# A FoX/RWKV-7 layer on one core: two products a slot later, one sum queued behind the solve, the last pair turned by VectorE

## The chip, the cores and the metric

The kernel runs on one core of one Trainium2 chip. The metric is the device time of one execution in microseconds (us), as the median of several runs. The core has five engines that work side by side, each through its own queue in order: TensorE (PE, with its weight loads shown as PEld), VectorE (DVE), ScalarE (ACT), GpSimd (POOL) and SyncE (SP). In this kernel SP issues almost all transfers (DMA) between the chip's memory and the core's on-chip memory.

## The reference

One layer for 256 frames of width 4096, all in float32:

```python
proj = x @ w_in                                # 256 x 4096 times 4096 x 14544
fox_out  = forgetting attention, 16 heads of 128, from q, k, v, f
r, kr, vr, wd, ad = token shift of the rwkv columns
decay = exp(-exp(-softplus(-(w0 + tanh(wd) @ w_up)) - 0.5))
a     = sigmoid(a0 + ad @ a_up)
y     = RWKV-7 scan, 32 heads of 64, in 4 chunks of 64 frames
h     = concat(fox_out, groupnorm(y) + bonus) * silu(z)
x     = layernorm(ALPHA * x + h @ w_out)
```

The two big products are the input projection and the output projection. Between them stand 16 attention heads and 32 small recurrent heads whose state goes from chunk to chunk.

## The kernel before

**Main work.** Every float32 operand is split into a high and a low part, and a product is three passes on TensorE: high times high, low times high, high times low (L147 to L149 for the input projection, L880 to L882 for the output). The input columns are taken in eight pairs of heads, n = 0 to 7, and four blocks of 512 columns, b = 0 to 3, for each pair: b = 0 holds r and k of the recurrent heads, b = 1 the values, b = 2 and b = 3 the q, k and gate columns of one attention head each. A weight tile holds two of the 32 row groups (512 KB). SP loads it (L218), ScalarE makes its high part (L141) and VectorE its low part (L142). Four raw tiles, four high parts and three low parts can be held at once.

**Side work and slots.** All the rest runs as Python generators that are advanced while the program is traced. `slot()` (L197) advances each generator by one `yield`, and the main loop calls it after every six wide matmuls, so a block of 512 columns has 32 slots and a pair 128. What a generator traces in a slot is queued on VectorE no earlier than the newest low part. `yield from wait(k)` lets k slots go by. The order on the engines is then fixed by a planner that goes by trace order and by when it reckons operands to be ready; the chip plays that order as it is. `keep_in_program_order(x)` pins x behind the instruction traced just before it on the same engine, whatever that is; `issue_after(y)` queues what is traced within behind y on y's engine.

**The generators.** `ahead` runs `prepare(i)` for the 16 column groups in turn; its first part, `front(i)` (L417), splits the up-projection weights (L420, L422), forms the LoRA product `lp` on TensorE (L428 to L430), and yields three times. `prepare(2n)` begins a slot after pair n-1 is done, and after `front` it waits until r and k of its group have come in (`rk`). `chain` runs `rwkv(n)` for the eight pairs: Gram products `gp` (L534), a triangular solve of 31 steps on VectorE (L601 and L604, one step in a slot), transfers of the solved blocks (`td` L611, `T` L613), the sum over values `vm` (L616), eight `SV` writes (L623), and then for the four chunks c: residual `rh` (L647), its copies `R` (L650, VectorE and ScalarE), `up` (L678), its copies `UV` (L681), and for c < 3 the state update `sp` (L687). The readout `yp` follows (L707, L709), then normalisation and gating into h.

**Turning blocks.** `unload(n, b)` (L796) brings a block from frames-by-columns to columns-by-frames. For all but two blocks VectorE transposes it in 32 x 32 pieces (L809), four transfers write it to memory (`turn`, L281) and, for an attention head, four bring it back as q, k and the two gates. For b = 2 and b = 3 of the last pair, TensorE transposes it instead (`tr`, L835) and ScalarE copies the result (L837). Then `fox(i)` runs the head: scores (L743, L744), softmax, transposed weights `pT` (L759), output (L764, L765).

**The output projection** begins while the last heads are still worked on. Fourteen weight tiles of output block 0 and fourteen of block 1 come first, with one slot for every six matmuls, 56 in all; then the last four row groups (28 to 31), which belong to the last pair. Row groups below 29 went to memory (`hd`) and come back (`h`, L855); 29 to 31 stay on the chip (`hl`, L382).

Of the kernel before, what the change touches and what calls it, by code (L numbers as in the profile page):

```python
# [14 lines left out]
ALU = mybir.AluOpType  # L15
AX = mybir.AxisListType

P = 128
S = 256
# [5 lines left out]
HD = 64  # L25
# [17 lines left out]
LAND = 3  # L43
# [41 lines left out]
def layer(ctx: ExitStack, tc: tile.TileContext, xt, xtok, w_main, w_lora, w_first, muv, w_o, up, par, mulora, fbias, lng, lnb, cst, out):  # L85
    nc = tc.nc
# [8 lines left out]
    def pst(name):  # L95
        return ps.tile([P, 512], F32, tag="ps", name=name)
# [34 lines left out]
    ident = cs[:, C_ID : C_ID + P]  # L131
# [26 lines left out]
    for n, (k0, k1) in enumerate(pieces):  # L158
        for k in range(k0, k1):
            t = xpool.tile([P, 2, S], F32R, tag=f"x{k}", name=f"x{k}")  # L160
# [29 lines left out]
    def wait(n):  # L190
        for _ in range(n):
            yield
# [87 lines left out]
    def issue(out, src):  # L280
        tc.keep_in_program_order(nc.sync.dma_start(out=out, in_=src))  # L281

    def turn(src, name, each=2):
        _, m, cols = src.shape
        d = dram.tile([cols // B, B, m, 4, B], F32, tag=f"dt{m}_{cols}", name=name, bufs=2)
        s = src.rearrange("p m (q t) -> p m q t", t=B)
        for a in range(4):
            issue(d[:, :, :, a, :].rearrange("q i m t -> i m q t"), s[B * a : B * (a + 1)])
            if a % each == each - 1:
                yield  # L290
        return d
# [109 lines left out]
    vs_ = {}  # L401
# [15 lines left out]
    def front(i):  # L417
        upt = ups[i]
        uph = rp.tile([LORA, 2, P], F32R, tag="uph", name=f"uph{i}")
        nc.scalar.copy(flat(uph), flat(upt))  # L420
        upl = rp.tile([LORA, 2, P], F32R, tag="upl", name=f"upl{i}")
        nc.vector.tensor_tensor(flat(upl), flat(upt), flat(uph).bitcast(F32), ALU.subtract)  # L422
        load_up(i + 1)
        yield
        lp = pst(f"lp{i}")
        for j in range(2):
            o = lp[:, j * S : (j + 1) * S]
            nc.tensor.matmul(o, uph[:, j, :], lr[:, j, 0, :], start=True, stop=False)  # L428
            nc.tensor.matmul(o, uph[:, j, :], lr[:, j, 1, :], start=False, stop=False)
            nc.tensor.matmul(o, upl[:, j, :], lr[:, j, 0, :], start=False, stop=True)  # L430
        tw = rt(f"tw{i}")
        nc.scalar.activation(tw, lp[:, :S], AF.Tanh, scale=0.5, bias=half[:, 0, i : i + 1])
        ta = rt(f"ta{i}")
        nc.scalar.activation(ta, lp[:, S:], AF.Tanh, scale=0.5, bias=half[:, 1, i : i + 1])
        yield
        nc.vector.tensor_scalar(tw, tw, -0.5 * DECAY, -0.5 * DECAY, ALU.mult, ALU.add)
        L = rt(f"L{i}")
        nc.vector.tensor_tensor_scan(L, cs[:, C_SCAN : C_SCAN + S], tw, 0.0, ALU.mult, ALU.add)
        eL = rp.tile([P, NCH, C + 1], F32, tag="eL", name=f"eL{i}")
        nc.gpsimd.memset(eL[:, :, 0:1], 1.0)  # L440
        nc.scalar.activation(eL[:, :, 1:], ch(L), AF.Exp)
        eI = t256("eI", f"eI{i}")
        nc.scalar.activation(eI, L, AF.Exp, scale=-1.0)
        yield
        am = t256("am", f"am{i}")
        nc.scalar.activation(am, ta, AF.Identity, scale=hka[:, 0, i : i + 1], bias=hka[:, 1, i : i + 1])
        ae = t256("ae", f"ae{i}")
        nc.vector.scalar_tensor_tensor(ae, ta, 1.0, eI, ALU.add, ALU.mult)
        return eL, eI, am, ae
# [70 lines left out]
    def rwkv(n):  # L520
# [8 lines left out]
        for u in range(2):  # L529
            for c in range(NCH):  # L530
                for j in range(2):
                    h = HALF[j]
# [4 lines left out]
        p, t = bks[n], vs_[n]  # L537
# [10 lines left out]
        for u in range(2):  # L548
            for j in range(2):
                h = HALF[j]  # L550
# [15 lines left out]
        for u in range(2):  # L566
            v = flat(BK[:, u, : NCH - 1, :])
# [25 lines left out]
        prod = rp.tile([P, 2, NJ, B], F32, tag="prod", name=f"prod{n}")  # L593
# [5 lines left out]
        for t, s in enumerate(range(B - 2, -1, -1)):  # L599
            w = B - 1 - s  # L600
            first = nc.vector.tensor_tensor(prod[:, :, :, s + 1 :], nb[:, :, s : s + 1, s + 1 :].to_broadcast([P, 2, NJ, w]), xc[:, :, :, s + 1 :], ALU.mult)  # L601
            if not t or not n:
                tc.keep_in_program_order(first)
            nc.vector.tensor_reduce(xc[:, :, :, s : s + 1], prod[:, :, :, s:], AX.X, ALU.add)  # L604
            next(other, None)
            if t % ROWS == ROWS - 1:
                yield
# [5 lines left out]
                nc.sync.dma_start(out=T[B * a : B * (a + 1), u], in_=td[u, a].rearrange("c r s -> r c s"))  # L613
        vm = rp.tile([P, 2, 2, 2], F32, tag="vm", name=f"vm{n}")
        vt = vs_[n].rearrange("p m (u j v) -> p m u j v", u=2, j=2)
        tc.keep_in_program_order(nc.vector.tensor_reduce(vm.rearrange("p m u j -> p (m u j)"), vs_[n].rearrange("p m (a v) -> p (m a) v", v=HD), AX.X, ALU.add))  # L616
        yield
        for j in range(2):
            o = HALF[1 - j]
# [51 lines left out]
        for c in range(NCH):  # L671
            if c:
                R = residual(c)
                yield
            yield
            upp = pst(f"up{n}_{c}")
            for u in range(2):
                nc.tensor.matmul(upp[:, u * C : (u + 1) * C], X[:, u, c, :], R[:, u, :], start=True, stop=True)  # L678
            uv = upp[:, : 2 * C].rearrange("p (u t) -> p u t", u=2)
            for j in range(2):  # L680
                (nc.vector.tensor_copy if j else nc.scalar.copy)(UV[j][HALF[j], :, c, :], uv[HALF[j]])  # L681
            yield
            if c == NCH - 1:
                break
            sp = pst(f"sp{n}_{c}")
            for u in range(2):
                nc.tensor.matmul(sp[:, u * P : (u + 1) * P], BKt[:, u, c, :], flat(UVt[:, u, c]), start=True, stop=True)  # L687
            for j in range(2):
                h = HALF[j]
                if c == 0:  # L690
                    nc.vector.tensor_copy(SV[j][h, :, 1, :], diagonal(sp, j))
                else:
                    nc.vector.tensor_tensor(SV[j][h, :, c + 1, :], diagonal(sp, j), sl[h], ALU.add)
            if c < NCH - 2:
                sl = rp.tile([P, 2, C], F32, tag="sl", name=f"sl{n}_{c}")
                for j in range(2):
                    for u in range(2):
                        nc.scalar.mul(sl[HALF[j], u], SV[j][HALF[j], u, c + 1, :], lc[HALF[j], u, c + 1 : c + 2])
            yield from wait(2)
# [96 lines left out]
    def unload(n, b, bk, vt):  # L796
        yield from wait(LAG)
        if b == 0:
            while n and 2 * n - 1 not in prepared:
                yield  # L800
        elif b == 2:
            while n and n - 1 not in done:
                yield
        last = n == G // 2 - 1 and b > 1
        if b == 3 and not last:
            yield from wait(BEHIND)
        if not last:
            for m in range(2):
                nc.vector.transpose(bk[:, m, :], bk[:, m, :])  # L809
            yield from wait(2)  # L810
            d = yield from turn(bk, f"bt{n}_{b}")
            unloading.clear()
            yield
        if b == 0:
            for u in range(2):
                i = 2 * n + u
                while n and n - 1 not in bonned:
                    yield
                raw = rp.tile([P, 2, S], F32, tag="s2", name=f"raw{i}")
                issue(raw, turned_back(d[8 * u : 8 * u + 8]))  # L820
                yield from wait(LAND)
                for j in range(2):
                    rk[i, j] = shifted(raw[:, j, :], j, i)
            return
        i = 2 * n + b - 2
        while i and i - 1 not in foxed:
            yield
        fq, fk = t256("fq", f"fq{i}"), t256("fk", f"fk{i}")
        zf, zr = t256("szf", f"zf{i}"), t256("szr", f"zr{i}", 2)
        if last:  # L830
            for h, pair in enumerate(((fq, fk), (zf, zr))):
                tr = pst(f"tr{h}")
                for t in range(2):
                    for m in range(2):
                        nc.tensor.transpose(tr[:, t * S + m * P : t * S + (m + 1) * P], bk[:, m, (2 * h + t) * P : (2 * h + t + 1) * P], ident)  # L835
                for t in range(2):
                    nc.scalar.copy(pair[t], tr[:, t * S : (t + 1) * S])  # L837
                yield
            unloading.clear()
        else:  # L840
            for j, t in enumerate((fq, fk, zf, zr)):
                issue(t, d[4 * j : 4 * j + 4].rearrange("b i m a t -> (b i) (m a t)"))
                if j % 2:
                    yield
            yield from wait(LAND - 1)
        nc.scalar.mul(fq, fq, FOX_SCALE)
        side(fox(i, fq, fk, vt))
        yield
        silu2(zf, f"f{i}")
        silu2(zr, f"r{i}")  # L850
# [267 lines left out]
```

## Time and profile before

| | |
|---|---|
| median of 3 runs | 1921.72 us (1921.52 to 1923.91) |
| profiled execution | 1921.7 us, of which the span from first to last instruction is 1919.5 us |
| TensorE clock granted | 0.998 of full speed |
| PE, DVE, ACT, POOL busy | 1906.1, 1375.6, 987.3, 259.1 us |
| moved by DMA | 420.04 MB, 219 GB/s on average |

How to read it: a row of the timeline has the start in us, the length, the engine, the source line, the operation, the tiles out<-in, the shape, and how many were merged; what stands in brackets at the end is the idle time before it and who ended it. Matmuls overlap: two neighbours that start 0.23 us apart are each shown as 0.39 us long, so a start-to-start distance, not a length, is what a matmul costs. A delay that is shorter than the overlap shows as no idle time.

### The profile page before, as it was taken

To read this page: it belongs to the slowest core of one execution; us is meant where nothing else is said; L and a number is where in the kernel's file an instruction comes from. 1 tells how busy PE (TensorE), PEld (TensorE's weight loads), DVE (VectorE), ACT (ScalarE), POOL (GpSimd) and SP (SyncE) were. 2 spreads that over 40 slices of the span, in tenths; PEclk is the share of its full clock that TensorE was granted. 3 is DMA by queue.
4 is the path that set the end of the run, shared out by engine and by line. 5 is a ranking of instruction groups with operands and counts; after the bars stand their busy time and mean duration, and the time that the engine had idled before them with its cause. 6 is when DMAs were issued, how large, how long until landed. Compare 5 with 4: busy or idle time off the path is not lost.

```text
span 1919.5 us, 27983 instructions
## 1 busy us (share of the span) xinstructions
PE 1906.1 (99%) x9785; PEld 1583.1 (82%) x9785; DVE 1375.6 (72%) x2355; ACT 987.3 (51%) x1543; POOL 259.1 (13%) x463
## 2 busy tenths in 40 slices
PE   9999999999999999999999999999999999999998
PEld 9878788888888888888888888888888878888886
DVE  7677768776876688677867786778677856755555
ACT  6554555456545644564456454645474554434333
POOL 0022012111310131013101300140013001000000
PEclk9999999999999999999999999999999999999999
DMA  9577667867686768677766776677667876766564
GB/s 344 154 232 230 193 188 229 242 202 208 209 249 194 225 204 244 195 217 217 237 199 213 223 232 203 212 225 223 206 211 221 276 257 231 253 200 202 186 203 165
DMA packets 269393, 420.04 MB, mean 219 GB/s; under 512 B 142338, under 2 KB 169364, under 8 KB 269252
## 3 DMA queue, kind: packets, MB, share of 16 engines
q1 hardware_dynamic: 268820, 417.58, 70.2%
q8 instruction: 76, 1.25, 0.3%
q10 hardware_dynamic: 432, 0.69, 0.1%
q14 instruction: 65, 0.53, 0.1%
HBM read 388.55 MB, written 29.64 MB: 218 GB/s over the span
## 4 chain that ended last, share of the span: by engine, by line
PE 96%; DVE 2%; DMA 1%; ACT 1%; issue 0%; SPq 0%; DVEq 0%; ACTq 0%
PE acc L147 24%; PE acc L149 23%; PE acc L148 23%; PE oacc L882 6%; PE oacc L880 6%; PE oacc L881 6%; PE gp L534 1%; PE rh L647 1%; PE up L678 1%; PE sp L687 1%; PE accl L149 1%; PE accl L147 1%; DMA w<-in_w_main_dram 1%; PE accl L148 0%; PE yp L709 0%
## 5 line engine op out<-in xcount | busy, mean ns | idle before, releaser
L759 POOL COPY pT<-lg 32x96 f32<-32x96 f32 x128 | 59.6, 466 | 406.7 <-DVE lg L755 402.0
L571 POOL COPY BKt<-BK 32x192 f32<-32x192 f32 x128 | 76.8, 600 | 55.2 <-DVE BK L568 50.2
L604 DVE TENSOR_REDUCE xc<-prod 128x8 f32<-128x16 f32 (+30 forms) x248 | 72.2, 291 | 5.5
L601 DVE TENSOR_TENSOR prod<-Nb,xc 128x8 f32<-128x8 f32 (+30 forms) x248 | 72.1, 291 | 3.6
L142 DVE TENSOR_TENSOR w_6l<-w,w_6h 128x1024 fp32r<-128x1024 f32 x31 | 39.8, 1283 | 40.6 <-ACT w_6h L141 23.4
L142 DVE TENSOR_TENSOR w_14l<-w,w_14h 128x1024 fp32r<-128x1024 f32 x31 | 38.0, 1225 | 39.4 <-ACT w_14h L141 33.3
L141 ACT CAST w_13h<-w 128x1024 fp32r<-128x1024 f32 x31 | 32.6, 1052 | 45.8 <-issue 12.3
L141 ACT CAST w_12h<-w 128x1024 fp32r<-128x1024 f32 x31 | 32.6, 1051 | 45.8 <-PE acc L148 26.5
L142 DVE TENSOR_TENSOR w_8l<-w,w_8h 128x1024 fp32r<-128x1024 f32 x31 | 37.8, 1220 | 25.4 <-ACT w_8h L141 17.2
L142 DVE TENSOR_TENSOR w_13l<-w,w_13h 128x1024 fp32r<-128x1024 f32 x31 | 38.3, 1234 | 23.6 <-ACT w_13h L141 12.1
L142 DVE TENSOR_TENSOR w_7l<-w,w_7h 128x1024 fp32r<-128x1024 f32 x31 | 37.9, 1222 | 20.5 <-ACT w_7h L141 8.0
L142 DVE TENSOR_TENSOR w_12l<-w,w_12h 128x1024 fp32r<-128x1024 f32 x31 | 38.9, 1256 | 18.8 <-ACT w_12h L141 10.3
L142 DVE TENSOR_TENSOR w_5l<-w,w_5h 128x1024 fp32r<-128x1024 f32 x31 | 39.7, 1282 | 16.8 <-PE acc L149 10.5
L142 DVE TENSOR_TENSOR w_11l<-w,w_11h 128x1024 fp32r<-128x1024 f32 x31 | 38.2, 1232 | 18.0 <-issue 12.4
L141 ACT CAST w_9h<-w 128x1024 fp32r<-128x1024 f32 x31 | 32.5, 1050 | 35.9 <-PE acc L148 25.5
L142 DVE TENSOR_TENSOR w_3l<-w,w_3h 128x1024 fp32r<-128x1024 f32 x31 | 37.9, 1222 | 18.0 <-ACT w_3h L141 10.2
L147 PE MATMUL acc<-w_5h,x 128*128 128x512 f32 x124 | 50.6, 408 | 0.0
L147 PE MATMUL acc<-w_8h,x 128*128 128x512 f32 x124 | 50.5, 408 | 0.0
L149 PE MATMUL acc<-w_2l,x 128*128 128x512 f32 x124 | 48.4, 391 | 1.4 <-DVE w_2l L142 1.4
L147 PE MATMUL acc<-w_15h,x 128*128 128x512 f32 x124 | 49.6, 400 | 0.0
L147 PE MATMUL acc<-w_11h,x 128*128 128x512 f32 x124 | 49.1, 396 | 0.4 <-ACT w_11h L141 0.4
L147 PE MATMUL acc<-w_9h,x 128*128 128x512 f32 x124 | 49.5, 399 | 0.0
(812 smaller groups left out, 6605.1 us busy)
## 6 DMA issues: line engine op xcount, KB each, us to landing
w<-in_w_main_dram SPq DMA_DIRECT2D x496, 512.0 KB
wo<-in_w_o_dram SPq DMA_DIRECT2D x128, 512.0 KB
bt<-bk SPq DMA_DIRECT2D x88, 128.0 KB
Nb<-nd SPq DMA_DIRECT2D x16, 512.0 KB
hd<-hl SPq DMA_DIRECT2D x29, 256.0 KB
h<-hd SPq DMA_DIRECT2D x29, 256.0 KB
wr<-in_w_first_dram SPq DMA_DIRECT2D x15, 384.0 KB
lr<-in_w_lora_dram SPq DMA_DIRECT2D x14, 336.0 KB
```

The lines of the kernel that those rows point to most:

```text
L141: nc.scalar.copy(hi[:, :n], src[:, :n])
L142: latest[0] = nc.vector.tensor_tensor(lo[:, :n], src[:, :n], hi[:, :n].bitcast(F32), ALU.subtract)
L147: nc.tensor.matmul(acc[:, :n], xs[k][:, 0, tt], hi[:, o : o + n], start=(k == 0), stop=False)
L148: nc.tensor.matmul(acc[:, :n], xs[k][:, 1, tt], hi[:, o : o + n], start=False, stop=False)
L149: nc.tensor.matmul(acc[:, :n], xs[k][:, 0, tt], lo[:, o : o + n], start=False, stop=(k == KT - 1))
L571: nc.gpsimd.tensor_copy(BKt[B * b : B * (b + 1), :, :, B * a : B * (a + 1)], BK[B * a : B * (a + 1), :, : NCH - 1, B * b : B * (b + 1)])
L601: first = nc.vector.tensor_tensor(prod[:, :, :, s + 1 :], nb[:, :, s : s + 1, s + 1 :].to_broadcast([P, 2, NJ, w]), xc[:, :, :, s + 1 :], ...
L604: nc.vector.tensor_reduce(xc[:, :, :, s : s + 1], prod[:, :, :, s:], AX.X, ALU.add)
L759: (nc.gpsimd.tensor_copy if b % 2 else nc.scalar.copy)(pT[B * b : B * (b + 1), :, B * a : B * (a + 1)], lg[B * a : B * (a + 1), :, B * b : ...
L880: nc.tensor.matmul(acc, ht[k][:, 0, tt], hi, start=(k == 0), stop=False)
L881: nc.tensor.matmul(acc, ht[k][:, 1, tt], hi, start=False, stop=False)
L882: nc.tensor.matmul(acc, ht[k][:, 0, tt], lo, start=False, stop=(k == KT - 1))
```

## The change

- `front(i)`: two slots instead of one go by before the LoRA product is traced.
- `rwkv(n)`: a further slot goes by before each state update `sp`, for chunks 0 to 2.
- `vm` is queued behind the last step of the solve on VectorE, not behind the instruction that happens to be traced before it.
- `unload(7, 2)` and `unload(7, 3)` take the way of the other blocks: VectorE transposes, four transfers out and four back. The TensorE transposes and ScalarE copies go. The wait of 13 slots that the other b = 3 blocks have is still left out for the last.

```diff
@@ front @@
         load_up(i + 1)
-        yield
+        yield from wait(2)
         lp = pst(f"lp{i}")
@@ rwkv @@
-            nc.vector.tensor_reduce(xc[:, :, :, s : s + 1], prod[:, :, :, s:], AX.X, ALU.add)
+            solved = nc.vector.tensor_reduce(xc[:, :, :, s : s + 1], prod[:, :, :, s:], AX.X, ALU.add)
...
-        tc.keep_in_program_order(nc.vector.tensor_reduce(vm.rearrange("p m u j -> p (m u j)"), vs_[n].rearrange("p m (a v) -> p (m a) v", v=HD), AX.X, ALU.add))
+        with tc.issue_after(solved.ins):
+            nc.vector.tensor_reduce(vm.rearrange("p m u j -> p (m u j)"), vs_[n].rearrange("p m (a v) -> p (m a) v", v=HD), AX.X, ALU.add)
...
             if c == NCH - 1:
                 break
+            yield
             sp = pst(f"sp{n}_{c}")
@@ unload @@
-        if not last:
-            for m in range(2):
-                nc.vector.transpose(bk[:, m, :], bk[:, m, :])
-            yield from wait(2)
-            d = yield from turn(bk, f"bt{n}_{b}")
-            unloading.clear()
-            yield
+        for m in range(2):
+            nc.vector.transpose(bk[:, m, :], bk[:, m, :])
+        yield from wait(2)
+        d = yield from turn(bk, f"bt{n}_{b}")
+        unloading.clear()
+        yield
...
-        if last:
-            for h, pair in enumerate(((fq, fk), (zf, zr))):
-                tr = pst(f"tr{h}")
-                for t in range(2):
-                    for m in range(2):
-                        nc.tensor.transpose(tr[:, t * S + m * P : t * S + (m + 1) * P], bk[:, m, (2 * h + t) * P : (2 * h + t + 1) * P], ident)
-                for t in range(2):
-                    nc.scalar.copy(pair[t], tr[:, t * S : (t + 1) * S])
-                yield
-            unloading.clear()
-        else:
-            for j, t in enumerate((fq, fk, zf, zr)):
-                issue(t, d[4 * j : 4 * j + 4].rearrange("b i m a t -> (b i) (m a t)"))
-                if j % 2:
-                    yield
-            yield from wait(LAND - 1)
+        for j, t in enumerate((fq, fk, zf, zr)):
+            issue(t, d[4 * j : 4 * j + 4].rearrange("b i m a t -> (b i) (m a t)"))
+            if j % 2:
+                yield
+        yield from wait(LAND - 1)
```

## The prediction

> **What bounds the kernel now.** I read the page's busy times first, then the chain that ended last, then TensorE's waits.
>
> ```profile
> PE 1906.1 (99%) x9785; PEld 1583.1 (82%) x9785; DVE 1375.6 (72%) x2355; ACT 987.3 (51%) x1543; POOL 259.1 (13%) x463
> PE 96%; DVE 2%; DMA 1%; ACT 1%; issue 0%; SPq 0%; DVEq 0%; ACTq 0%
> ```
>
> ```profile
> PE acc L149 <- DVE w_2l L142: 1.4, 1, 1.4
> ```
>
> TensorE is busy 99% and carries 96% of the chain. The time is its queue: the wide passes, the small products between them, and the few moments in which it stands still. So each edit is worth what it takes out of or adds to the start-to-start distances on TensorE; VectorE (72%), ScalarE (51%) and the transfers matter only where they come late for it. The longest listed wait on other work is this one of 1.4 us; but the list is not all, since a delay below 0.16 us (0.39 long, 0.23 apart) hides in the overlap.
>
> **A. The TensorE transposes of the last pair go.**
>
> ```profile
> 1501.09 0.39 PE L149 MATMUL acc<-w_1l,x 128*128 128x512 f32 x1
> 1501.32 0.60 PE L835 MATMUL tr<-cs,bk 128*128 128x128 f32 x4
> 1501.67 0.48 PE L147 MATMUL acc<-w_1h,x 128*128 128x512 f32 x1
> 1501.99 0.40 PE L148 MATMUL acc<-w_1h,x 128*128 128x512 f32 x1
> ```
>
> From 1501.09 to the second wide pass after the group is 0.90; two plain distances would be 2 x 0.227 = 0.45. So four transposes cost 0.45 us. Two blocks in two halves make four such groups: 4 x 0.45 = **1.8 us less**, on the bounding engine, without doubt. [...]
>
> **B. `sp` a slot later.** A group of four 128-column products costs 0.45 when it waits for nothing (A). For `sp`:
>
> ```profile
> 1366.73 0.40 PE L149 MATMUL acc<-w_4l,x 128*128 128x512 f32 x1
> ```
>
> ```profile
> 1367.72 0.39 PE L148 MATMUL acc<-w_4h,x 128*128 128x512 f32 x1
> ```
>
> ```profile
> 1383.25 0.40 PE L149 MATMUL acc<-w_9l,x 128*128 128x512 f32 x1
> ...
> 1384.29 0.39 PE L148 MATMUL acc<-w_9h,x 128*128 128x512 f32 x1
> ```
>
> ```profile
>   DVE UV L681: 3.5, 13
> ```
>
> These are the wide passes around a group, in two places. The distances are 0.99 and 1.04, so the groups cost 0.54 and 0.59: 0.09 and 0.14 more than 0.45. The last line, the idle time before `sp`, says that 13 of the 24 groups wait for the `UV` copy. A slot is 6 x 0.227 = 1.36 us, far more, so the wait ends: 13 x 0.11 = **1.4 us less** (0 if it moves to the next product, 1.8 at 0.14 each). With `sp` go its `SV` writes on VectorE and the scaled copies on ScalarE, no transfer; the steps behind keep their distances, and each pair's chain gets 3 slots longer.
>
> **C. `lp` a slot later.**
>
> ```profile
>   DVE upl L422: 1.3, 6
> ```
>
> Six products waited 1.3 us in all for VectorE's low part of the up-projection. In B the waits showed half in the distances (13 x 0.11 of 3.5), so I take **0.4 us less**, between 0 and 1.3.
>
> **D. `vm` behind the solve.** In pair 0 it now runs among the solve's steps, and its `SV` writes with it:
>
> ```profile
> 208.17 0.68 DVE L616 TENSOR_REDUCE vm<-vs 128x8 f32<-128x512 f32 x1
> ...
> 214.66 1.22 DVE L142 TENSOR_TENSOR w_2l<-w,w_2h 128x1024 fp32r<-128x1024 f32 x1
> ```
>
> ```profile
> 214.09 0.39 PE L148 MATMUL acc<-w_2h,x 128*128 128x512 f32 x1
> 215.93 0.50 PE L149 MATMUL acc<-w_2l,x 128*128 128x512 f32 x1 [1.45 <-DVE w_2l L142]
> ```
>
> TensorE stood 1.84 - 0.23 = 1.6 us for a low part queued behind `vm` (0.68) and the eight `SV`. With these behind the solve the low part can come sooner; or the planner puts as much other work ahead of it. Between 0 and 1.6 I take **0.8 less**. ScalarE's copies of `SV` follow the same way, and no transfer does; in pair 7 `vm` already comes after the solve.
>
> **E. The stall of pair 7.**
>
> ```profile
> 1574.02 0.39 PE L880 MATMUL oacc<-wo_8h,h 128*128 128x512 f32 x1
> 1575.31 0.66 PE L678 MATMUL up<-R,X 128*128 128x64 f32 x4 [0.90 <-ACT R L650]
> ```
>
> ```profile
> 1575.00 0.26 ACT L650 COPY R<-rh 64x128 f32<-64x128 f32 x1
> ```
>
> Here `R` comes at 1575.00 on ScalarE, which the last attention head's copies and a cast have held before; 1.29 - 0.23 = 1.1 us. That head comes 7 slots later by the new transfers, the recurrent chain 9 to 12, so this meeting dissolves or another takes its place: 0 to 1.1, I take **0.6 less**.
>
> **F. What the change adds.**
>
> ```profile
> L809 DVE STREAM_TRANSPOSE bk<-bk x44: 660/694/714, 73.9 to 1412.8; 128x512 f32<-128x512 f32 x44
> ```
>
> VectorE gets four of these transposes (median 694 ns), ScalarE loses eight copies; neither is near its limit. SP gets eight writes, which wait for these transposes, and eight reads, which wait for the writes; weight loads, `h` and the head's `nb` are queued behind them:
>
> ```profile
> 1378.68 3.23 SPq L281 DMA_DIRECT2D bt<-bk  x4
> ...
> 1384.53 0.33 SPq L281 DMA_DIRECT2D fq<-bt  x1
> ...
> 1385.85 0.43 SPq L281 DMA_DIRECT2D zr<-bt  x1
> ```
>
> So 3.2 + 1.8 = 5.0 us of SP's queue for each block. For block (7, 2) it falls where pairs 0 to 6 have the same without a wait. For (7, 3) it falls at 1549 to 1557, among the weight loads of the output projection, and there the chain matters. Counted in the code from one pair's end to the next, `prepare` starts after 1 slot, then 14 for each of two heads, 5, 14, the solve's 31, 15, 18 to `yp`, 11 to the end: 123 of a pair's 128, so 5 are spent waiting for r and k. Now 2 come from `lp` and 3 from `sp`: 128, no slack. What pair 0 is late by (4 slots) and what later pairs used to win back stays: 12 slots from pair 2 on at the end of a chain, 9 at the solve's end. No extra slots are run for it: the last recurrent head ends 12 slots later, 12 x 1.36 = 16 us and the side work in them, and there is room, since its last part is ready at 1601.9 and the first of the last row groups is used at 1633.7:
>
> ```profile
> L382 DVE TENSOR_TENSOR hl<-h,hl x4: 416/418/425, 1532.1 to 1601.5; 128x256 fp32r<-128x256 f32 x4
> ```
>
> ```profile
> 1633.74 0.39 PE L880 MATMUL oacc<-wo_14h,hl 128*128 128x512 f32 x1
> ```
>
> But the solved blocks of pair 7 go through SP at least 9 x 1.36 = 12 us later too, next to the transfers of (7, 3). Now they leave a gap in the weight loads:
>
> ```profile
> 1528.13 0.33 SPq L218 DMA_DIRECT2D wo<-in_w_o_dram  x1
> ...
> 1537.74 0.43 SPq L218 DMA_DIRECT2D wo<-in_w_o_dram  x1
> ```
>
> ```profile
> 1546.52 1.23 DVE L142 TENSOR_TENSOR wo_2l<-wo,wo_2h 128x1024 fp32r<-128x1024 f32 x1 [2.47 <-ACT wo_2h L141]
> ```
>
> ```profile
> 1550.70 0.39 PE L882 MATMUL oacc<-wo_2l,h 128*128 128x512 f32 x1
> ```
>
> After 9.6 us without a load the low part is ready 2.95 us before its pass. Put 5.0 us of further transfers on top, and TensorE waits at most 5.0 - 2.95 = 2.0; at least 0, and not less, since it waits for no weights there now. I take **1.0 more**.
>
> Sum: -1.8 - 1.4 - 0.4 - 0.8 - 0.6 + 1.0 = -4.0. The profiled execution is 1921.7 (span 1919.5 and 2.2 around it), the median 1921.72, so the one stands for the other: **1917.7 us**. About 0.2%, 3.8 us, is what a measurement of this kernel tells from no change.
>
> **Rivals.**
>
> *The transfers of the last block come late.* All of F's 2.0 is paid, and D and E do not come, since the stretch is as crowded as before: -1.8 - 1.4 - 0.4 + 2.0 = -1.6, 1920.1. For it speaks how full the transfers are when a block is turned, and where (7, 3) would go:
>
> ```profile
> 1380.00:1385.00 5.00, 5.00 (x27) 4.03 (x27) 2.34 (x5) 1.57 (x3) 0.00 (x0) 1.00 0.93 129
> ```
>
> ```profile
> 1545.00:1550.00 5.00, 5.00 (x56) 4.00 (x55) 1.93 (x2) 4.15 (x9) 0.00 (x0) 1.00 1.04 407
> ```
>
> The last two columns are the DMA share and GB/s: writing a turned block takes 93% of the engines at 129 GB/s, and five microseconds of that would meet a stretch that is full at 407. Against it: weight tiles are held four deep. [...]
>
> *The waits only move.* `sp`, `R` or a low part waits elsewhere, since 12 slots shift every meeting of the chain with the attention heads: A comes, a third of B to E (3.2 / 3 = 1.1) and F: -1.8 - 1.1 + 1.0 = -1.9, 1919.8. That the slots and the queueing do nothing at all is its end: -1.8 + 1.0, 1920.9. For it speaks that B to E hang on meetings of tenths of a microsecond; against it, that a slot (1.36) is ten times the waits in B.
>
> *Slower: the low part after the solve.* In pairs 1 to 6 `vm` and four of the `SV` run among the solve's last steps, and four behind them (here pair 6):
>
> ```profile
> 1339.89 0.67 DVE L616 TENSOR_REDUCE vm<-vs 128x8 f32<-128x512 f32 x1
> ...
> 1343.85 0.98 DVE L623 SCALAR_TENSOR_TENSOR SV<-vm,vs 64x128 f32<-64x128 f32 x4
> 1344.87 1.23 DVE L142 TENSOR_TENSOR w_14l<-w,w_14h 128x1024 fp32r<-128x1024 f32 x1
> ```
>
> ```profile
> 1346.45 0.39 PE L149 MATMUL acc<-w_14l,x 128*128 128x512 f32 x1
> ```
>
> The low part is ready at 1346.10, 0.35 before its pass. If the solve ends no sooner and `vm` and four `SV` (0.67 + 0.98 = 1.65 us) still come ahead of that part, it is 1.65 - 0.35 = 1.3 late, six times: +7.8 - 3.6 (A to C) = +4.2, 1925.9. It decides for slower from (3.8 + 3.6) / 6 = 1.2 us late. Against it: the same work in another order ends when it did, unless the steps wait for each other.
>
> **How the numbers follow.** Forecast 0.48 (its own range 1914.1, all of A to E at their far ends and no F, to 1917.9); late transfers 0.22; moved waits 0.20; slower 0.10. Faster is the first, 0.48; same the next two, 0.42; slower 0.10. The range leaves out the slower rival and the far end of the forecast: 1915.2 to 1921.5.
>
> **What would show it.** No `tr` groups; no idle time before `sp` and 0.45 for each; `lp` waiting less than 1.3; no stall near 214 and none at `up` in pair 7; `vm` after the solve in all eight pairs; the last `hl` near 1620. Wrong would be: `acc` or `oacc` waiting for a low part once in every pair, a weight cast waiting for DMA after 1545 until TensorE starves, or `up` waiting for `R`.

## The result and the profile after

The changed kernel is slower: 1929.32 us (median, 1928.31 to 1930.36) against 1922.16 us for the kernel before in the same comparison, a ratio of 1.0037 with a 95% interval of 1.0024 to 1.005. The forecast was 1917.7 us, with a range from 1915.2 to 1921.5. The profiled execution took 1929.84 us, its span 1928.1 us. One execution of experiment 3 below, 2724.46 us long at a granted clock of 0.654, is left out, and the median given there is that of the other nine.

The busy times and the chain that ended last, from the page of the changed kernel:

```profile
PE 1907.0 (99%) x9769; PEld 1584.4 (82%) x9769; DVE 1397.0 (72%) x2359; ACT 983.6 (51%) x1535; POOL 266.3 (14%) x463
PE 94%; DVE 2%; DMA 2%; ACT 1%; SPq 1%; issue 0%; DVEq 0%; ACTq 0%
```

TensorE has 16 matmuls fewer (9785 before), as step A said. In the chain it gave up two points, and SyncE's queue (SPq), which had 0%, now has 1%.

Where the time went is seen when the same piece of work is found in both traces. The first wide pass of the block (7, 3), before and then after (start, length, engine, line):

```profile
1497.23 0.39 PE L147 MATMUL acc<-w_0h,x 128*128 128x512 f32 x1
```

```profile
1493.88 0.39 PE L147 MATMUL acc<-w_0h,x 128*128 128x512 f32 x1
```

and the first pass of the output projection with the tile `wo_4`, second column block, before and after:

```profile
1605.18 0.39 PE L880 MATMUL oacc<-wo_4h,h 128*128 128x512 f32 x1
```

```profile
1613.72 0.39 PE L870 MATMUL oacc<-wo_4h,h 128*128 128x512 f32 x1
```

Up to 1494 us the changed kernel was 3.4 us ahead. At 1613 us it was 8.5 us behind, and that stays to the end. So 11.9 us were lost in 120 us, just where the two turned blocks are. Between the two points TensorE has the same products to do in both kernels, but for the 16 transposes and two products of `sp`. TensorE's own list of waits in the changed kernel (what was waited for, us in total, times, longest):

```profile
PE oacc L870 <- ACT wo_7h L141: 3.2, 1, 3.2
PE oacc L870 <- ACT wo_5h L141: 2.1, 1, 2.1
...
PE acc L149 <- DVE w_5l L142: 1.2, 1, 1.2
...
PE fop L766 <- POOL pT L761: 0.9, 1, 0.9
PE oacc L872 <- DVE wo_5l L142: 0.5, 1, 0.5
```

Four of these five lie in the stretch. Three of the four are waits for weight tiles of the output projection; the other, `fop` at 1531 us, waits for `pT` from GpSimd. Behind ScalarE's casts of the weight tiles stands a transfer (timeline of ScalarE, idle time in brackets):

```profile
1557.98 1.04 ACT L141 CAST wo_5h<-wo 128x1024 fp32r<-128x1024 f32 x1 [0.59 <-DMA wo<-in_w_o_dram]
...
1567.69 1.04 ACT L141 CAST wo_7h<-wo 128x1024 fp32r<-128x1024 f32 x1 [5.98 <-DMA wo<-in_w_o_dram]
```

The load for `wo_7h` came late because of what stands ahead of it in SyncE's queue (timeline of SyncE, changed kernel, start and length of the issue):

```profile
1538.22 0.33 SPq L218 DMA_DIRECT2D wo<-in_w_o_dram  x1
1538.64 0.38 SPq L845 DMA_DIRECT2D h<-hd  x1
1545.01 0.79 SPq L611 DMA_DIRECT2D td<-xc  x2
1545.89 0.38 SPq L845 DMA_DIRECT2D h<-hd  x1
1546.37 0.38 SPq L218 DMA_DIRECT2D wo<-in_w_o_dram  x1
1546.86 3.69 SPq L613 DMA_DIRECT2D T<-td  x8
...
1552.11 0.35 SPq L218 DMA_DIRECT2D wo<-in_w_o_dram  x1
...
1553.78 0.37 SPq L218 DMA_DIRECT2D wo<-in_w_o_dram  x1
1554.24 3.00 SPq L281 DMA_DIRECT2D bt<-bk  x2
1557.33 3.01 SPq L845 DMA_DIRECT2D h<-hd  x1
1560.40 1.28 SPq L281 DMA_DIRECT2D bt<-bk  x2
1561.78 0.92 SPq L845 DMA_DIRECT2D h<-hd  x1
1562.79 0.60 SPq L218 DMA_DIRECT2D wo<-in_w_o_dram  x1
```

From 1538 to 1563 us only five weight loads are issued; the kernel before used seven tiles in 25 us here (`wo_0` from 1543.1 to `wo_7` at 1568.1). The first gap is `td`, which waits for the end of the solve. Then come the eight `T`, and 3.7 us after them the turned block (7, 3), `bt`, with a gap of 9.0 us from one weight load to the next. `wo_7` is the load behind that gap. The load of `wo_5` is issued at 1552.11, ahead of the turned block, and its cast starts only 5.9 us later (the median of these loads is 4.5 us from issue to landing). So the gap of `td` and `T` had already used up the stock, and the writes did not have to stand ahead of `wo_5` in the queue for it to be late.

The last piece stands in the granted clock (windows of the changed kernel: us, busy time and count of PE, PEld, DVE, ACT, POOL, then clock, DMA share, GB/s):

```profile
1565.00:1570.00 5.00, 1.82 (x5) 0.67 (x3) 1.23 (x2) 1.40 (x2) 0.00 (x0) 0.88 0.98 351
...
1568.00:1569.00 1.00, 0.21 (x1) 0.21 (x2) 0.23 (x1) 1.00 (x2) 0.00 (x0) 0.92 1.00 383
1569.00:1579.00 10.00, 9.94 (x53) 7.06 (x54) 8.24 (x13) 4.28 (x8) 1.52 (x2) 0.50 0.85 300
1579.00:1580.00 1.00, 1.00 (x6) 0.83 (x5) 0.00 (x0) 0.00 (x0) 0.00 (x0) 0.96 0.51 127
```

After the wait for `wo_7h` TensorE ran at half clock for 10.2 us, which cost up to 5.1 us by estimate: wide passes start 0.43 us apart there, and 0.23 us elsewhere. The kernel before has 1.00 throughout this stretch; the same window there:

```profile
1569.00:1579.00 10.00, 9.10 (x47) 7.09 (x46) 5.63 (x11) 5.99 (x17) 3.03 (x8) 1.00 0.40 131
```

So the account of 11.9 us: waits 3.2 + 2.1 + 0.9 + 0.5 = 6.7, a further 0.4 for `wo_3h` at 1549.5, less the 0.9 that `up` waited in the kernel before (step E), the clock 5.1, the transposes saved -1.8 (A); together 9.5. The other 2.4 us are not assigned; each of the five waits hides up to 0.16 us more in the overlap (0.39 us long, 0.23 apart), and the list leaves short waits out.

What the other steps foretold did come. The waits ahead of `sp` in the changed kernel, as the answer on its line gives them:

```profile
L689 PE MATMUL sp<-UV,BKt x96: 271/275/347, 237.7 to 1602.2; 128*128 128x128 f32 x96
L689 PEldq EVENT_SEMAPHORE  x1: 51/51/51, 258.0 to 258.0; - x1
its engine sat idle before it (us, times) until:
  issue: 0.4, 1
  DVE UV L682: 0.2, 1
```

One group waits 0.2 us for `UV`; before, thirteen waited 3.5 us. No `lp` product waits (six did), and in pair 0 the low part `w_2l` starts at 209.76, ahead of `vm`; it started at 214.66. The stall of `up` in pair 7 is gone too. A smaller stall, 1.2 us for `w_5l` at 324 us, is new; `vm` does not run near it.

```profile
209.76 1.22 DVE L142 TENSOR_TENSOR w_2l<-w,w_2h 128x1024 fp32r<-128x1024 f32 x1
...
217.25 0.68 DVE L617 TENSOR_REDUCE vm<-vs 128x8 f32<-128x512 f32 x1
```

### The profile page after: what moved, and what is told of

Same layout as the page of the kernel before. It is cut to its first block, busy times and chain, and to the rows that moved or that the text cites. A ratio compares the mean times of both kernels' runs of the same rounds, so it can differ in the third digit from the quotient of the medians.

```text
span 1928.1 us, 27991 instructions
## 1 busy us (share of the span) xinstructions
PE 1907.0 (99%) x9769; PEld 1584.4 (82%) x9769; DVE 1397.0 (72%) x2359; ACT 983.6 (51%) x1535; POOL 266.3 (14%) x463
## 4 chain that ended last, share of the span: by engine, by line
PE 94%; DVE 2%; DMA 2%; ACT 1%; SPq 1%; issue 0%; DVEq 0%; ACTq 0%
PE acc L147 23%; PE acc L149 23%; PE acc L148 23%; PE oacc L872 6%; PE oacc L870 6%; PE oacc L871 6%; PE rh L648 1%; PE gp L534 1%; PE up L679 1%; DMA w<-in_w_main_dram 1%; DMA wo<-in_w_o_dram 1%; PE sp L689 1%; PE accl L149 0%; PE accl L148 0%; PE accl L147 0%
## 5 line engine op out<-in xcount | busy, mean ns | idle before, releaser
L142 DVE TENSOR_TENSOR w_0l<-w,w_0h 128x1024 fp32r<-128x1024 f32 x31 | 38.5, 1243 | 33.6 <-ACT w_0h L141 24.4
L142 DVE TENSOR_TENSOR w_10l<-w,w_10h 128x1024 fp32r<-128x1024 f32 x31 | 38.0, 1224 | 26.1 <-ACT w_10h L141 11.6
L142 DVE TENSOR_TENSOR w_15l<-w,w_15h 128x1024 fp32r<-128x1024 f32 x31 | 38.1, 1229 | 19.4 <-issue 17.5
L142 DVE TENSOR_TENSOR w_9l<-w,w_9h 128x1024 fp32r<-128x1024 f32 x31 | 38.0, 1226 | 18.7 <-ACT w_9h L141 8.4
L141 ACT CAST w_8h<-w 128x1024 fp32r<-128x1024 f32 x31 | 32.6, 1052 | 37.1 <-DMA w<-in_w_main_dram 19.1
L149 PE MATMUL acc<-w_5l,x 128*128 128x512 f32 x124 | 48.5, 391 | 1.2 <-DVE w_5l L142 1.2
L147 PE MATMUL acc<-w_14h,x 128*128 128x512 f32 x124 | 49.5, 399 | 0.0
L147 PE MATMUL acc<-w_6h,x 128*128 128x512 f32 x124 | 49.1, 396 | 0.0
L147 PE MATMUL acc<-w_1h,x 128*128 128x512 f32 x124 | 49.0, 395 | 0.0
L147 PE MATMUL acc<-w_0h,x 128*128 128x512 f32 x124 | 49.0, 395 | 0.0
```

The source lines that it names most:

```text
L141: nc.scalar.copy(hi[:, :n], src[:, :n])
L142: latest[0] = nc.vector.tensor_tensor(lo[:, :n], src[:, :n], hi[:, :n].bitcast(F32), ALU.subtract)
L147: nc.tensor.matmul(acc[:, :n], xs[k][:, 0, tt], hi[:, o : o + n], start=(k == 0), stop=False)
L149: nc.tensor.matmul(acc[:, :n], xs[k][:, 0, tt], lo[:, o : o + n], start=False, stop=(k == KT - 1))
```

## The experiments

The median of the kernel before lies between 1922.2 and 1923.0 us in the four comparisons, so ratios to it are the safer measure; a difference of medians from two comparisons carries up to 0.8 us of that. "Gross" below means with the 1.8 us of step A added back, as predicted; that term was not measured by itself.

**1 to 4: which part of the change.** Experiment 1 keeps the slots and `vm` and gives the last pair back to TensorE. Experiment 2 is the reverse: the kernel before with the transfers alone.

```diff
@@ 1, on the changed kernel: unload as it was before @@
...
+        if last:
+            for h, pair in enumerate(((fq, fk), (zf, zr))):
+                tr = pst(f"tr{h}")
...
@@ 2, on the kernel before: unload as changed, the rest untouched @@
-        if not last:
-            for m in range(2):
-                nc.vector.transpose(bk[:, m, :], bk[:, m, :])
...
@@ 3, on 1: TensorE turns (7, 3) alone @@
-        last = n == G // 2 - 1 and b > 1
+        last = n == G // 2 - 1 and b == 3
@@ 4, on 1: TensorE turns (7, 2) alone; (7, 3) still does not wait 13 slots @@
-        last = n == G // 2 - 1 and b > 1
-        if b == 3 and not last:
+        last = n == G // 2 - 1 and b == 2
+        if b == 3 and n < G // 2 - 1:
```

> The changed kernel with the last pair turned by TensorE again: both slots and the queueing of vm stay. Theory 1 (the 16 new transfers of the last pair starve the weight loads): the loss is gone and the gain that the changed kernel had by the start of block (7, 3), 3.4 us, stays: about 1918.5. Theory 2 (the recurrent chain, 9 to 12 slots later, puts the solved blocks of pair 7 among the weight loads of the output projection, with or without turned blocks): still slow, 1926 to 1930. Theory 3 (only both together fill SP's queue): like theory 1, about 1918.5.

> The kernel before with the last pair turned by VectorE and transfers, no slot added, vm as before. Theory 1: 1922 less 1.8 for the TensorE transposes, plus the 12 us that the changed kernel lost between 1493 and 1613: about 1930. Theory 2 and theory 3: 1920.2, the 1.8 gained and nothing lost.

> The changed kernel with block (7, 3) turned by TensorE again, so only (7, 2) goes by transfers. If the writes and reads of (7, 3) among the weight loads are the cause: 1922 - 3.4 - 0.9 = about 1917.7. If the backlog begins with (7, 2), whose turn already makes the casts wait for weights from 1505 on: 1925 or more. Theory 2: 1926 to 1930.

> The changed kernel with block (7, 2) turned by TensorE again, so only (7, 3) goes by transfers. If (7, 3) is the cause: about 1929, as the changed kernel. If the backlog begins with (7, 2): about 1918 to 1920. Theory 2: 1926 to 1930.

| | median us | ratio to the kernel before (95%) |
|---|---|---|
| 1 slots and `vm`, no transfers | 1918.70 | 0.9979 (0.9969 to 0.9988) |
| 2 transfers alone | 1924.38 | 1.0009 (0.9999 to 1.0018) |
| 3 changed, block (7, 2) alone by transfers | 1922.44 | 0.9996 (0.9987 to 1.0006) |
| 4 changed, block (7, 3) alone by transfers | 1923.78 | 1.0006 (0.9997 to 1.0015) |
| the changed kernel | 1929.32 | 1.0037 (1.0024 to 1.005) |

The slots and `vm` gain 4.3 us. The whole loss belongs to the transfers, but not to them by themselves: with the old chain they cost 1.4 us (3.2 gross), with the later chain 1929.3 - 1918.7 = 10.6 us (12.4 gross). Experiment 2 met neither of the values expected for it; what it asked for is an interaction. Each block alone costs 3.7 and 5.1 us on the later chain, so neither is the sole cause, and neither run met a value expected for it. Executions of 2 spread from 1921.72 to 1927.54 us and those of 4 from 1921.47 to 1928.25; the profiled execution of 4 is its longest.

Why block (7, 2) costs anything, 40 us ahead of the output projection's first wait, the traces show. Its turn makes the weights late for ScalarE's cast, in the changed kernel; without it, in experiment 1, the same cast waits for no transfer:

```profile
1509.60 1.05 ACT L141 CAST w_8h<-w 128x1024 fp32r<-128x1024 f32 x1 [3.82 <-DMA w<-in_w_main_dram]
```

```profile
1507.74 1.05 ACT L141 CAST w_8h<-w 128x1024 fp32r<-128x1024 f32 x1 [1.66 <-PE acc L148]
```

The low parts on VectorE come late with the casts, and the solve's steps are queued between them. So with (7, 2) on SyncE's queue the solve of pair 7 ends some 5 us later: `td` is issued at 1545.2 in experiment 3 and at 1545.0 in the changed kernel, but at 1539.2 in experiment 1 and 1540.2 in experiment 4. In experiment 3 TensorE then waits 1.5 + 0.5 us for `wo_5` and has 3.4 us at half clock, with no turned block near.

**5 to 8: what in the stretch makes it costly.** Three theories: A, SyncE's queue, in which weight loads stand behind other transfers; B, the number of bytes in small elements, from whatever queue; C, the chain that comes 9 to 12 slots later and so brings its transfers next to the turned block. (In what was expected of experiment 5, C is another theory: that the attention head of this block ends last. Its 1935 us did not come.)

```diff
@@ 5, on the changed kernel: (7, 3) waits 13 slots, as the b = 3 blocks of other pairs do @@
-        if b == 3 and not last:
+        if b == 3:
             yield from wait(BEHIND)
@@ 6, on the changed kernel: transfers of (7, 2) and (7, 3) from GpSimd's queue @@
-        tc.keep_in_program_order(nc.sync.dma_start(out=out, in_=src))
+        tc.keep_in_program_order((queue or nc.sync).dma_start(out=out, in_=src))
...
+        queue = nc.gpsimd if last else nc.sync
...
@@ 7, on 2: rwkv(7) alone starts 9 slots later @@
+        if n == G // 2 - 1:
+            yield from wait(9)
@@ 8, on the changed kernel: row group 28 stays on chip @@
-FAR = 29
+FAR = 28
```

> The changed kernel, but the turn of the block (7,3) waits 13 slots more, as the same block of every earlier pair does (some 20 us at 1.5 us a slot), so that its 3.0 us writes no longer stand among the state chain's td and T transfers and the wait of td for the solve's end. Theory A, the writes meet the state chain's transfers in SyncE's in-order queue and the weights behind them come late: most of what the block (7,3) costs (the changed kernel less the run with the block (7,2) turned alone, 1929.3 - 1922.6 = 6.7 us) comes back: 1922 to 1925 us. Theory B, the transfers of both blocks are too many bytes in small elements for the stretch, wherever they stand: the same backlog arises 20 us later, 1927 to 1931 us. Theory C, what matters is that the forget head of this block ends last: its product then starts 20 us later, beyond the state chain's end: 1935 us or more.

> The changed kernel with the sixteen transfers of the two last blocks issued from GpSimd's queue in place of SyncE's; the same bytes, the same slots. Theory A (SyncE's queue in order holds the weight loads behind the writes and the waiting reads): the weights come as in the kernel without these transfers, 1918 to 1922 us, and the waits of the casts for w_o of up to 6 us at 1567 go. Theory B (the DMA engines are filled by the 3.0 us writes, from whatever queue): 1926 to 1931 us, with the waits of the casts still there. Between them, GpSimd's own work (pT of the forget heads) is queued behind its waiting DMA issues: some 2 to 3 us of waits of fop for pT, 1921 to 1925 us.

> The kernel before with the transfers alone (1924.4 us), but with the state chain of the last pair started 9 slots later, as far as the changed kernel's stands later at its solve. No wait of sp, lp or vm is changed. Theory C (the transfers became dear because the chain comes 9 to 12 slots later and meets them): 1928 to 1933 us, 4 to 8 us over the run without the delay, with casts that wait for w_o between 1560 and 1580 us and a lower granted clock there. Rival (the later chain does not matter, it is the moved state update itself, or vm, that the transfers disturb): 1923 to 1926 us.

> The changed kernel without the store and the load of row group 28: it stays on chip like the groups 29 to 31, so that no 3.0 us h<-hd load stands in SyncE's queue at 1557 us between the two blocks' transfers. Theory A (queue, the waiting h load holds the weights of w_o behind it): 2 to 4 us less, 1925 to 1927.5 us, and the cast of wo_7h waits less than 3 us (5.98 us in the changed kernel). Theory B (bytes): the store and the load are 2 of some 12 such transfers: 1 us less at most, 1928 to 1929.5 us.

| | median us | ratio (95%) | last pair's `td` at | `bt` of (7, 3) at |
|---|---|---|---|---|
| 2 transfers alone | 1924.38 | 1.0009 (0.9999 to 1.0018) | 1534.6 | 1559.3 |
| 5 (7, 3) 13 slots later | 1922.75 | 0.9999 (0.999 to 1.0008) | 1543.5 | 1571.4 |
| 6 from GpSimd's queue | 1920.63 | 0.9987 (0.9978 to 0.9997) | 1540.1 | 1546.6, other queue |
| 7 old chain, 9 slots late | 1936.57 | 1.0072 (1.0057 to 1.0087) | 1551.0 | 1560.8 |
| 8 row group 28 kept | 1927.64 | 1.0029 (1.0017 to 1.004) | 1542.7 | 1551.4 |
| the changed kernel | 1929.32 | 1.0037 (1.0024 to 1.005) | 1545.0 | 1554.2 |

Experiment 7 shows C: nothing but 9 slots of delay for one pair turns 1924.4 into 1936.6, more than was expected (the granted clock fell to 0.50 twice there, for 6.8 us each time). In the three longest kernels of the table (7, 8 and the changed one) the turn follows `td` by 8.7 to 9.8 us in SyncE's queue; in 2 and 5 it follows by 25 and 28 us. Experiment 5 met what A expected of it: with (7, 3) alone moved away, 6.6 of the 10.6 us are back.

Experiment 6 shows A against B. The same bytes go in the same slots, and 8.7 of the 10.6 us are back, as A expected (1918 to 1922 us; B expected 1926 to 1931). In its profiled execution, the fastest of ten, all are (span 1916.3, that of experiment 1 is 1916.1). The solve of pair 7 is no longer held up either: `td` is at 1540.1. Issues on GpSimd's queue in experiment 6, then the weight loads on SyncE's:

```profile
1546.60 3.28 POOL L281 DMA_DIRECT2D bt<-bk  x4 [17.03 <-DVE bk L810]
1556.75 0.57 POOL L281 DMA_DIRECT2D fq<-bt  x1 [6.87 <-DMA bt<-bk]
```

```profile
1548.91 0.57 SPq L218 DMA_DIRECT2D wo<-in_w_o_dram  x1
...
1551.89 0.60 SPq L218 DMA_DIRECT2D wo<-in_w_o_dram  x1
...
1553.83 5.97 SPq L218 DMA_DIRECT2D wo<-in_w_o_dram  x3
```

The weights pass beside the writes, and the engines move more. The stretch of 20 us in the changed kernel and in experiment 6 (columns as above):

```profile
1550.00:1570.00 20.00, 14.15 (x82) 9.35 (x80) 6.71 (x8) 4.91 (x6) 0.00 (x0) 0.97 0.92 267
```

```profile
1550.00:1570.00 20.00, 17.39 (x134) 12.93 (x133) 10.78 (x16) 9.86 (x15) 3.66 (x6) 1.00 0.95 344
```

344 GB/s in place of 267: the bytes did not hold the kernel at 1929 us. What they still cost is not separated: by the medians experiment 6 stays 1.9 us above experiment 1, and waits of 1.5 and 0.9 us for `wo_5h` and `wo_6h` remain. The other queue alone saved 8.7 us by the medians: on SyncE's queue the weight loads stood behind the writes (9.0 us from one load to the next), on the other queue beside them (at most 3.0 us), with the DMA share at 0.95.

Experiment 8 gave 1.7 us, with overlapping intervals; not told from nothing, and TensorE still waits 3.0 us for `wo_7h`, where the changed kernel has 3.2. How long the cast itself waits there, less than 3 us as expected by A, no row shows. The experiment undid a reading of mine, that the 3.01 us of the `h<-hd` load at 1557 was its wait for its own store. Without that load another `h` load stands there and takes as long (experiment 8, SyncE):

```profile
1551.42 2.44 SPq L281 DMA_DIRECT2D bt<-bk  x2
1553.96 3.24 SPq L845 DMA_DIRECT2D h<-hd  x1
1557.25 1.29 SPq L281 DMA_DIRECT2D bt<-bk  x2
```

So in these two traces the issue of the `h` load behind the first two writes takes 3.01 and 3.24 us, whichever load it is; what holds it was not tried.

**9 to 11: the three small edits alone**, each on the kernel before.

```diff
@@ 9, rwkv @@
+            yield
             sp = pst(f"sp{n}_{c}")
@@ 10, front @@
-        yield
+        yield from wait(2)
         lp = pst(f"lp{i}")
@@ 11, rwkv @@
+            solved = nc.vector.tensor_reduce(xc[:, :, :, s : s + 1], prod[:, :, :, s:], AX.X, ALU.add)
...
+        with tc.issue_after(solved.ins):
+            nc.vector.tensor_reduce(vm.rearrange("p m u j -> p (m u j)"), vs_[n].rearrange("p m (a v) -> p (m a) v", v=HD), AX.X, ALU.add)
```

> The kernel before with the state update sp one slot later and nothing else (the chain of a pair goes from 123 to 127 slots, there is no turn by transfers in the last pair). By step B of the prediction: 1.4 us less in the span (1918.1 us against 1919.5), with sp groups near 0.45 us instead of those that waited. By the rival 'the waits only move': a span of 1919.5 us, with the stall at up or at the weights of a step behind it. A delay of the chain that costs by itself: a span over 1920.5 us.

> The kernel before with the LoRA product lp one slot later and nothing else. By step C of the prediction: 0.4 us less in the span (1919.1 us; 0 to 1.3 us less). Rival: nothing, 1919.5 us.

> The kernel before with the sum over values (vm) queued behind the solve and nothing else. By step D of the prediction: the stall of 1.4 us for w_2l at 214 us goes and 0.8 us remain as gain (1918.7 us in the span; 0 to 1.6 us less). Rival, the stall only moves to the next weight tile that VectorE makes late: 1919.5 us and a stall of 1 us or more at another w tile.

| | median us | ratio (95%) | span us |
|---|---|---|---|
| 9 `sp` alone | 1924.56 | 1.0006 (0.9996 to 1.0016) | 1922.7 |
| 10 `lp` alone | 1920.84 | 0.9985 (0.9975 to 0.9994) | 1919.4 |
| 11 `vm` alone | 1921.37 | 0.9992 (0.9983 to 1.0002) | 1918.9 |

By the medians the three give +1.5, -2.2 and -1.6, together -2.3; as one they gave -4.3. `sp` alone gains nothing that can be measured: a group of `sp` a slot later adds 0.45 us (median, in the changed kernel) to the distance of the wide passes around it, against 0.53 before, but in experiment 9 another low part, `w_1l`, comes late beside `w_2l`, which was late before (waits of TensorE in experiment 9):

```profile
PE acc L149 <- DVE w_2l L142: 1.3, 1, 1.3
...
PE acc L149 <- DVE w_1l L142: 1.3, 1, 1.3
PE accl L147 <- ACT wl1h L141: 1.1, 1, 1.1
```

The last line lies at the start of the kernel, where the edit has not yet acted. The span of 1922.7 lies where a delay of the chain was expected to cost by itself (over 1920.5), but with 1.1 us of it from that start and 1.3 from `w_1l` this is not shown. (The chain has 126 slots here, not the 127 that were expected: 123 and three.) With `vm` alone the stall at `w_2l` is gone from the list and the span is 0.6 us shorter, near the 0.8 expected. For `lp` alone the trace is 2.0 us ahead up to 1882 us, but its span shows 0.1: in the tail the granted clock fell to 0.50 at 1908.8, 2.7 us earlier than in the kernel before (1911.5). One profiled execution is therefore no measure for a term of 1 us here.

**12: both remedies.** Experiment 6 with row group 28 kept on the chip.

> The changed kernel with the last two blocks' transfers on GpSimd's queue (that run: 1920.6 us, span 1916.3) and with row group 28 kept on chip. If the waits that are left there (wo_5h 1.5 us, wo_6h 0.9 us) come from SyncE's queue and DMA engines that the store and load of row 28 fill: 1.5 to 2.4 us less in the span, 1914 to 1915 us, and the fastest kernel of the study. If they come from the transfers' bytes, which stay: 1916 us.

1918.51 us, ratio 0.9978 (0.9969 to 0.9987). The wait for `wo_5h` that was to go is still there (2.6 us, 1.5 in experiment 6), so the expected cause is not borne out. The span of 1919.9 misses the 1914 to 1915 expected, but this profiled execution is the longest of ten. By the medians the kernel is 2.1 us faster than experiment 6, with intervals that overlap, so the step is not clear of noise. Together with experiment 1 (1918.70) it is the fastest kernel seen, and both are faster than the kernel before and the changed one. So turning the last pair by transfers, even with both remedies, shows no gain over leaving it to TensorE.

## Why the prediction was wrong

- **A** was right: 16 matmuls fewer and no `tr` group. That the saving is 1.8 us was not measured by itself.
- **B, C, D**: the waits went as foretold, and the three edits together are worth 4.3 us by experiment 1, where the prediction had 1.4 + 0.4 + 0.8 + 0.6 = 3.2 with E. The sum came out near, but as single terms they do not hold, so that is in part luck: B alone gives no gain, C alone more than its 0.4 and its upper bound of 1.3 (2.2 us by the medians), D alone 1.6 by the medians against 0.8, with an interval that includes no change.
- **E**: the stall of `up` is gone in the changed kernel and in experiment 1. Its worth was not measured by itself.
- **F is the step that failed**, the cost of the new transfers. It saw the right place ("among the weight loads of the output projection, and there the chain matters"), the 9 slots, and the solved blocks "next to the transfers of (7, 3)". Then it put 5.0 us of issue on top of the gap of the kernel before and subtracted 2.95 us of stock: "TensorE waits at most 5.0 - 2.95 = 2.0". Measured: 12.4 us gross for both blocks, 6.2 times the upper bound. Three things were wrong in that one line. First, 5.0 us was the price of eight transfers as pair 6 issued them; here the stretch from the first to the last write alone is 7.4 us (1554.24 to 1561.68), since an `h` load stuck for 3.0 us between them. Second, the gap of `td` and `T` does not lie under the new one but ahead of it, so the stock was already used up when the turn began: between 1538 and 1563 us five tiles came, where the kernel before used seven in as long a time. Third, the stall of TensorE cost more than its length, since 10.2 us at a granted clock of 0.50 followed it: 5.1 us by estimate.
- "For block (7, 2) it falls where pairs 0 to 6 have the same without a wait" was wrong as well: that block alone costs 3.7 us on the later chain. The prediction moved the solve's end by the slots alone; the late weights of this turn move it by some 5 us more (experiments 1, 3 and 4).
- The rival "the transfers of the last block come late" had this mechanism, priced with F's 2.0 us, and so ended at 1920.1. Of the signs named for being wrong, a weight cast that waits for DMA after 1545 until TensorE starves is what came. The rival on the slower side (a low part behind the solve in each pair) did not come: `vm` was no cause of loss in any pair.
- The last `hl` comes at 1626.3, not near 1620; that cost nothing, since it is first needed near 1642.

## What to carry to other kernels

The tiles loaded ahead of the bounding engine are a stock, and each gap in the queue that fills it must be costed with the gaps next to it: here the same transfers cost 1.4 us where the turn of (7, 3) follows `td` by 25 us (experiment 2), and 10.6 us where it follows by 9 (the changed kernel). Ask of a later chain which queue entries it brings together, and try a queue of its own for a transfer that waits or is slow to issue before calling bytes the limit (here it brought back 8.7 of the 10.6 us). An edit that relieves one wait may show nothing until the next wait is moved along with it; that is how I read `sp` alone, and no run shows it.

## What was not expected of the hardware

In these traces the granted clock of TensorE falls to 0.50 after a stall and stays there for 3.4, 6.8 or 10.2 us. Read in windows of 0.2 to 2.5 us, the low stretches between 1545 and 1590 us are 10.2 us in the changed kernel, 3.4 in experiment 2, 3.4 in 3, 3.4 and 10.2 in 4, 6.8 twice in 7, and 10.2 in 8; none in the kernel before and in 1, 5, 6, 9 and 12. By estimate half of such a stretch is lost, 1.7 us of one of 3.4. One of these, in experiment 2:

```profile
1549.00:1550.00 1.00, 0.94 (x4) 0.47 (x3) 0.92 (x2) 0.05 (x1) 0.00 (x0) 0.92 0.98 367
1550.00:1553.00 3.00, 3.00 (x8) 2.30 (x7) 2.09 (x3) 2.25 (x3) 0.00 (x0) 0.50 1.04 408
1553.00:1554.00 1.00, 1.00 (x5) 0.82 (x4) 0.69 (x1) 0.51 (x1) 0.00 (x0) 0.87 1.00 328
```

In the 3.4 us before the eight falls TensorE was still busy for 0.24 us at least (the changed kernel) and 2.09 at most (an upper bound, for the second fall in experiment 7). What triggers a fall was not shown: experiment 2 has one after 3.4 us with 1.81 us of work, while a stretch of 3.4 us with at most 1.37 us of work (experiment 5 from 1555.0) passed without.
